# Other start addresses in SBUF for the pools of a decoder-layer kernel

## The chip, the cores and the metric

The kernel runs as one program on one core of a Trainium2 chip. The metric is device time in microseconds (us) of one execution, the median of several runs; lower is better. The core's engines are TensorE (PE: matmuls; PEld: its loads of the stationary operand), VectorE (DVE), ScalarE (ACT), GpSimd (POOL) and SyncE (SP, which issues the DMAs here).

## What is computed

One layer of a conditioned decoder on 256 tokens of 2048 channels, all in float32. Both halves are normalised (RMS norm) and shifted, scaled and gated by vectors made from a conditioning vector `c`:

```python
mod = silu(c) @ w_ada + b_ada                       # 2048 x 12288
h = rms_norm(x) * (1 + scale1) + shift1
z = h @ w_in + b_in                                 # 2048 x 11312: q, k, v, gates, GLU
y_attn = nsa_attention(q, k, v, gates) @ w_nsa_out  # compressed, selected and window branch
y_conv = conformer_conv(a_glu)                      # causal depthwise convolution of 31 taps, pointwise
x = x + gate1 * ((g0 * y_attn + g1 * y_conv) @ w_out)
h2 = rms_norm(x) * (1 + scale2) + shift2
s = (h2 @ w_q) . sub_keys; choose 16 of 16384 experts for each of 8 heads
out = x + gate2 * sum_e gate_e * gelu(h2 . u_e) * v_e
```

The kernel does the last line densely: `h2` against all 16384 rows of `u`, then the coefficients (zero where an expert is not chosen) against all rows of `v`. So nearly all of its work is one long row of matrix products whose weights (512 KB a transfer, some 500 MB in all) come from HBM once.

## The kernel before

**The stream of weights.** The class `Stream` (L130 to L217) takes the weights chunk by chunk. A chunk is 1024 float32 columns of each of 128 partitions. SP loads it into one of four tiles `raw` (L147). For each half of it, a piece of 512 columns, ACT writes the rounded part `hi` (L153, type float32r) and DVE the rest `lo = raw - hi` (L159, float32r); there are five `hi` and four `lo` tiles. `raw`, `hi` and `lo` are the pool `stream`.

**The products of a piece.** What is multiplied is split in the same way, so a product is three matmuls: high x high, high x low, low x high. In the projections (L200 to L202) the weights are the stationary operand (128x128, loaded by PEld) and the activations, 256 tokens, are the moving one: twelve matmuls of 256 columns a piece. In the stage of `u` (L213, L215) high and low part of `h2` lie side by side and are moved together, 512 columns, against `hi`, then the high part alone, 256 columns, against `lo`: eight matmuls a piece. In the stage of `v` (L1310 to L1312) it is the other way round: the coefficients `chi`, `clo` are stationary and 512 columns of `hi` or `lo` are moved: six matmuls a piece. Rows of the profile name the output, then the moving operand, then the stationary one: `acc<-hhi,lo` moves `hhi` over the stationary `lo`.

**The order of the work.** It is written out by hand (`manual_schedule`). `Stream.piece` (L170) keeps the splits up to three pieces ahead of the products, issues the products and then lets each job that runs beside them take a step or a fraction of one: the convolution, the adaLN vectors (`ada_steps`, which loads 256 KB tiles `adaw` and sums them on DVE, L383), the norms, attention, the top-16 search, the scatter of the gates.

**The stages** by the moving operand on PE, in us of the trace: 0 to 148 shift, scale and norm, with plain float32 products (`zb<-hr,w`, L339, no split); 148 to 561 projections of `h` (`hhi`, `hlo`) with convolution, then attention beside them; 561 to 645 `yhi`, `ylo`; 645 to 834 `ohi`, `olo` and the last of `h` in turn, with the adaLN jobs; 834 to 939 the output projection of `mhi`, `mlo`; 939 to 1037 `uhi`, `ulo` and then `h2` against the query weights of the experts; 1037 to 1794 `h2` against `u`; 1794 to 2501 the stage of `v`.

**Memory.** Pools are laid out as they are opened: `const`, `stream` and others from the low end of a partition upwards, those with `side="right"` from the high end downwards. A tile starts at the next multiple of 32 bytes. No address is written in the kernel; sizes and order give them.

Of the kernel before, what the change touches and what calls it, by code (L numbers as in the profile page):

```python
# [9 lines left out]
F32 = mybir.dt.float32  # L10
# [23 lines left out]
BIG = 1e30  # L34
# the gates are split into two halves of 11 bits, exactly, after this factor
GS = 32768.0
LOW = -3.0e38

# columns of the packed vectors
VEC = {}  # L40
# [7 lines left out]

# columns of the constants
CID, CONE, CMASK, CIOTA, CCM, CVAL, CI16, CEPS = 0, 128, 256, 384, 512, 542, 543, 559  # L50
# [22 lines left out]
def build(nc, tc, d):  # L73
# [18 lines left out]
    const = P("const")  # L92
    stream = P("stream")
    dram = ctx.enter_context(tc.tile_pool(name="dram", bufs=1, space=DRAM))
    ctx.enter_context(tc.manual_schedule())
# [21 lines left out]
    def col_sum(ps, a):  # L117
        """ps[m, :] = sum over partitions of a[:, m], in each of 128 columns."""
        pe.matmul(ps, a, ones, start=True, stop=True)
# [4 lines left out]

    # ---- the stream of weights: 4 KiB chunks of each partition, split exactly into high and
    # low parts in pieces of 512 columns, ahead of the products ----
    AHEAD = 3

    class Stream:
# [11 lines left out]
        def prefetch(self, to):  # L141
            """Low parts up to piece `to`, high parts up to the next one."""
            last = 2 * len(self.chunks) - 1
# [21 lines left out]
        def piece(self, mm):  # L165
            """The products of the next piece, and a step of each job that runs beside them."""
            self.prefetch(self.at + AHEAD)
            mm(*self.parts.pop(self.at))
            self.at += 1
            self.step()  # L170
# [10 lines left out]
        def add(self, gen, rate=1.0):  # L181
            """A job: `rate` steps of it beside each piece."""
            job = [gen, rate, 0.0]
            self.jobs.append(job)
            return job
# [7 lines left out]
        def proj(self, bank, nk, xhi, xlo, evac):  # L193
            """ps[n, t] = sum_k W[k, n] x[k, t] with the next chunks of the stream."""
            ps = bank()
            for k0 in range(0, nk, 4):
                def mm(hi, lo):
                    for j in range(4):
                        k, o = k0 + j, j * 128
                        pe.matmul(ps, hi[:, o:o + 128], xhi[:, k], start=(k == 0), stop=False)  # L200
                        pe.matmul(ps, hi[:, o:o + 128], xlo[:, k], start=False, stop=False)  # L201
                        pe.matmul(ps, lo[:, o:o + 128], xhi[:, k], start=False, stop=(k == nk - 1))  # L202
                self.piece(mm)
            return self.add(evac(ps))

        def proj2(self, bank, nk, x, evac):
            """The same with x = [high | low]; ps[:, 0] + ps[:, 1] are the sums."""
            ps = bank()
# [16 lines left out]
    G0, G1, QT, GATE = 43, 59, 27, 26  # L225
    # row tiles of v that are taken bank by bank
    LAST = 8
# [25 lines left out]

# [1 line left out]
    sp.dma_start(vec, d["vec"])  # L255
# [12 lines left out]

    # silu(c); halved biases for sigmoid through tanh: gate, glu (16), merge gates (32), all from b_gate on
    ctmp = const.tile([128, 16], F32, name="ctmp")  # L270
# [4 lines left out]
    ve.tensor_scalar(hvec, vec[:, g0:g0 + 49], 0.5, None, op0=OP.mult)  # L275
    gkq = const.tile([128, 3], F32, name="gkq")
    ve.tensor_scalar(gkq, v("gk", 0, 3), v("gq"), None, op0=OP.mult)

# [14 lines left out]
    def first_h(k):  # L293
        """shift1, scale1 and h of 128 channels."""
        acc = xp.tile([128, 2, 256], F32, name="acc1", tag="acc1", bufs=2)
# [40 lines left out]
    def first_z(k):  # L336
        """Their share of the first column tiles."""
        for n in range(14):
            pe.matmul(zb[n // 2][:, n % 2], ws[k][n // 7][:, n % 7], hr[k], start=(k == 0 and n % 2 == 0),  # L339
                      stop=(k == KT - 1), skip_group_check=True)  # L340
# [14 lines left out]

# [1 line left out]
    adap = [None]  # L357

    def ada_steps(groups, bank):
        """mod columns of groups of 512 channels."""  # L360
        pool = adap[0]
# [42 lines left out]

# [1 line left out]
    cpool = P("cpool", side="right")  # L406
# [54 lines left out]
    def conv_steps():  # L461
# [11 lines left out]
        yield  # L473
        # by tokens: mean and variance of the channels, from transposes
        yT = glu.rearrange("p c t -> p (c t)")[:, 0:2 * CT * 128].rearrange("p (a b) -> p a b", a=4)
# [62 lines left out]

    # keys and values
    adap[0] = P("adap")  # L540
# [19 lines left out]
    def gelu_small(out, ps):  # L560
        # 0.5 x (1 + tanh(sqrt(2/pi) (x + 0.044715 x^3)))
        x = cp.tile([64, 128], F32, name="gx", tag="gx", bufs=2)[0:60]
# [67 lines left out]
    def sums_steps(src, o, step):  # L630
        """By token: the sums of src[:, token]^2 over the partitions, into ssq[:, o + half * step]."""
        p2 = gen_bank([128, 2, 128])
# [33 lines left out]
    def q_evac(h):  # L666
        def f(ps):
# [4 lines left out]
            yield  # L672
            # columns by group, query tile, head
            yield from sums_steps(q, (h // 4) * 8 + h % 4, 4)
# [37 lines left out]

    # 1/sqrt of the mean squares of the keys; of the queries, with the scale of the scores
    def k_norm_steps():
# [26 lines left out]

# [1 line left out]
    P.close("gpool", "cp")  # L743
# [5 lines left out]
    def attention(g, qt):  # L749
# [25 lines left out]

        # compressed keys
        pk = gen_bank([128, HPG, NG, 24])
# [10 lines left out]
        yield  # L788
        # selected blocks (all of them) and window
        maxima(0, s0)  # L790
# [16 lines left out]
        yield  # L807
        # gate / sum
        ve.reciprocal(sums, sums)
# [50 lines left out]

    # the convolution's projection
    def conv_out(n):
# [30 lines left out]

# [1 line left out]
    ada[1] = 0.9  # L895
# [19 lines left out]

# [1 line left out]
    # h2 = rs2[t] u + shift2 with u = x1 (1 + scale2) g2; the first projections take u and, as two more  # L917
    # columns, shift2, since u needs no sum over all channels
    UC = T + 2
# [5 lines left out]
    rs2 = np_.tile([128, T], F32, name="rs2")  # L925
    hgate = np_.tile([128, 16], F32, name="hgate")
    uhi = np_.tile([128, KT, UC], F32R, name="uhi")
    ulo = np_.tile([128, KT, UC], F32R, name="ulo")
    x1d = dram.tile([128, 2, D], F32, name="x1d")
    ss2 = np_.tile([128, 2, 4], F32, name="ss2")  # L930
    r2 = np_.tile([128, 2], F32, name="r2")
    summed = []

    def x1_out(q):
        """Four channel tiles of x1, by tokens, to DRAM."""
        for tt in range(2):
# [32 lines left out]
    def h2_steps():  # L969
        """The columns of shift2; then rs2 and h2."""  # L970
        while not summed:
# [42 lines left out]

# [1 line left out]
    def u_bank(shape, tag, bufs=2):  # L1016
# [25 lines left out]
    def pairs(gen):  # L1042
        """Two steps of a generator as one."""
        while next(gen, S) is not S:
# [49 lines left out]
    def top_steps():  # L1094
        for h in range(PH):
            while h not in heads:
                yield
            yield from head_top(heads[h], h)
        # softmax of the chosen scores
        G4 = [128, 2, PH, TOPK]  # L1100
# [8 lines left out]
        yield  # L1109
        # slots on partitions  # L1110
        for nm, src in (("I1T", I1), ("I2T", I2), ("low", gates)):
# [77 lines left out]
    def g_steps():  # L1189
        """The gates of four tokens at a time, scattered over all experts and into C."""  # L1190
        I1T, I2T, high, low = (slot_t[n] for n in ("I1T", "I2T", "high", "low"))
# [64 lines left out]
    def coef(i1):  # L1256
        """The parts of an expert row tile's coefficients."""
        if i1 <= HALF:
# [10 lines left out]

# [1 line left out]
    coefs = {0: coef(0)}  # L1271
# [5 lines left out]
    def gate2_steps():  # L1277
        """The terms of gate2, by rows of w_ada."""
        todo = [(g, k) for g in range(4) for k in range(KT)]
# [37 lines left out]
    def gate2_sums():  # L1317
        """The first sums to SBUF; gate2 of all tokens through their banks."""
        for tt in range(2):
# [43 lines left out]
    S.finish(end)  # L1363
    P.close("ps_mix", "vp", "gg", "cb", "stream", "const")
    ctx.close()


def layout(inputs):
    """The inputs in the order in which the chip reads them."""
    a = {n: np.asarray(x) for n, x in inputs.items()}  # L1370
# [5 lines left out]
    def tiles(w, nk):  # L1376
        # [K, N] -> [N/128][128 k][nk][128 n]
        n = w.shape[1] // 128
# [22 lines left out]
    wa = a["w_ada"][0]  # L1401
    # by 128 channels: [channel tile][row within its tile][row tile][shift, scale][channel]
    wa1 = wa[:, 0:4096].reshape(KT, 128, 2, KT, 128).transpose(3, 1, 0, 2, 4).reshape(KT, 128, KT, 256)
# [27 lines left out]
```

## Time and profile before

| | |
|---|---|
| three runs | 2503.33, 2505.09, 2512.18 us (median 2505.09) |
| profiled execution, first to last instruction | 2506.6 us |
| busy share | PE 98%, PEld 86%, DVE 78%, ACT 57% |
| DMA | 540 MB, mean 216 GB/s |
| granted PE clock | 0.998 of full speed (mean) |
| chain that ended last | PE 86%, DMA 6%, DVE 6% |

The three runs and the span of the profiled execution lie within 0.4% of each other. How to read it: "busy" of PE overlaps from one matmul to the next, since matmuls are pipelined and their ends are modelled; what a matmul really takes of PE's time is the distance from its start to the start of the next one in the timeline.

### The profile page before, as it was taken

Reading aid. Unit: us, or ns where it says so; the run is one execution under the profiler, and the core shown is the slowest. Engines: PE = TensorE matmul, PEld = TensorE weight load, DVE = VectorE, ACT = ScalarE, POOL = GpSimd, SP = SyncE. Lnnn points to the kernel's source line nnn. Section 1 sums busy time; section 2 is a strip of 40 time slices with the busy share of each in tenths; the row PEclk is TensorE's granted clock in tenths of the full one; section 3 lists DMA queues with packets and bytes.
Section 4 is the critical chain, followed back from the end, with each engine's and each line's share of the span. In section 5 each row is a group of like instructions: output and inputs, shape, how many; then the busy total and the mean of one; then the engine's idle time right before and its main releaser. Section 6 shows DMA issues by size and latency. Waiting matters only on the chain.

```text
span 2506.6 us, 44063 instructions
## 1 busy us (share of the span) xinstructions
PE 2456.7 (98%) x15324; PEld 2165.1 (86%) x15324; DVE 1944.4 (78%) x4136; ACT 1421.1 (57%) x3198; POOL 0.2 (0%) x4
## 2 busy tenths in 40 slices
PE   7999999999999999999999999999999999999999
PEld 6899999888989999988888888888888888888887
DVE  7979886888777876899987888888655556666665
ACT  1045456776444456555568888887555555555554
POOL 0000000000000000000000000000000000000000
PEclk9999999999999999999999999999999999999999
DMA  9955566645988885555555555555555557777766
GB/s 382 395 190 194 178 194 196 202 155 188 308 288 289 291 280 194 177 185 186 190 183 175 175 173 173 176 170 176 185 191 190 192 190 253 243 237 241 238 208 195
DMA packets 171553, 540.48 MB, mean 216 GB/s; under 512 B 18753, under 2 KB 19009, under 8 KB 171073
## 3 DMA queue, kind: packets, MB, share of 16 engines
q1 hardware_dynamic: 171330, 537.67, 64.9%
q8 instruction: 120, 1.97, 0.3%
q14 instruction: 103, 0.84, 0.1%
HBM read 533.41 MB, written 4.19 MB: 214 GB/s over the span
## 4 chain that ended last, share of the span: by engine, by line
PE 86%; DMA 6%; DVE 6%; issue 1%; SPq 0%; ACT 0%; DVEq 0%
PE ps_acc L213 19%; PE ps_acc L215 10%; PE acc L200 7%; PE acc L202 7%; PE acc L201 7%; DMA adaw<-in_w_ada_dram 5%; DVE acc L307 2%; PE ps_o L1312 2%; PE ps_t L1312 2%; PE ps_s L1312 2%; PE ps_acc L1312 2%; PE ps_o L1311 2%; PE ps_s L1311 2%; PE ps_t L1311 2%; PE ps_acc L1311 2%; PE ps_o L1310 2%
## 5 line engine op out<-in xcount | busy, mean ns | idle before, releaser
L153 ACT CAST hi<-raw 128x512 fp32r<-128x512 f32 x1548 | 954.4, 621 | 835.3 <-PE acc L201 237.0
L159 DVE TENSOR_TENSOR lo<-raw,hi 128x512 fp32r<-128x512 f32 x1548 | 1062.2, 688 | 389.3 <-ACT hi L153 79.9
L213 PE MATMUL ps_acc<-h,hi 128*128 128x512 f32 x2048 | 731.3, 400 | 0.0
L215 PE MATMUL ps_acc<-h,lo 128*128 128x256 f32 x2048 | 575.1, 281 | 0.0
L213 PEld LDWEIGHTS ps_acc<-h,hi 128*128 128x128 f32 x2048 | 385.2, 188 | 91.1
L215 PEld LDWEIGHTS ps_acc<-h,lo 128*128 128x128 f32 x2048 | 384.7, 188 | 0.0
L200 PE MATMUL acc<-hhi,hi 128*128 128x256 f32 x1200 | 347.0, 289 | 0.0
L202 PE MATMUL acc<-hhi,lo 128*128 128x256 f32 x1200 | 335.0, 279 | 3.4 <-DVE lo L159 3.1
L201 PE MATMUL acc<-hlo,hi 128*128 128x256 f32 x1200 | 334.2, 278 | 0.0
L200 PEld LDWEIGHTS acc<-hhi,hi 128*128 128x128 f32 x1200 | 225.8, 188 | 6.3 <-issue 5.3
L202 PEld LDWEIGHTS acc<-hhi,lo 128*128 128x128 f32 x1200 | 226.2, 188 | 5.2 <-DVE lo L159 5.2
L201 PEld LDWEIGHTS acc<-hlo,hi 128*128 128x128 f32 x1200 | 226.3, 189 | 3.2 <-issue 3.1
L383 DVE SCALAR_TENSOR_TENSOR ada<-adaw,sc_c,ada 128x512 f32<-128x512 f32 x180 | 134.4, 747 | 51.4 <-DMA adaw<-in_w_ada_dram 51.3
L469 DVE SCALAR_TENSOR_TENSOR cacc<-glu,dwh,cacc 128x256 f32<-128x256 f32 x240 | 105.3, 476 | 0.0
L1202 ACT ACTIVATE Ahi<-ohA,high 128x128 f16<-128x128 f16 x256 | 100.5, 392 | 0.0
L339 PE MATMUL zb<-hr,w 128*128 128x256 f32 x448 | 100.4, 382 | 0.0
L1202 ACT ACTIVATE Alo<-ohA,low 128x128 f16<-128x128 f16 x256 | 99.0, 387 | 0.0
L339 PEld LDWEIGHTS zb<-hr,w 128*128 128x128 f32 x448 | 85.0, 192 | 11.1
L307 DVE SCALAR_TENSOR_TENSOR acc<-wa,sc_c,acc 128x256 f32<-128x256 f32 x224 | 91.4, 477 | 0.0
L202 PE MATMUL acc<-ohi,lo 128*128 128x256 f32 x256 | 72.7, 284 | 6.8 <-DVE lo L159 6.7
L202 PE MATMUL acc<-mhi,lo 128*128 128x256 f32 x256 | 73.6, 287 | 3.2 <-DVE lo L159 3.2
L200 PE MATMUL acc<-mhi,hi 128*128 128x256 f32 x256 | 73.1, 286 | 0.0
(367 smaller groups left out, 4388.3 us busy)
## 6 DMA issues: line engine op xcount, KB each, us to landing
raw<-in_u_dram SPq DMA_DIRECT2D x256, 512.0 KB, 3.7
raw<-in_v_dram SPq DMA_DIRECT2D x256, 512.0 KB, 4.4
raw<-in_w_in_dram SPq DMA_DIRECT2D x150, 512.0 KB, 4.2
adaw<-in_w_ada_dram SPq DMA_DIRECT2D x192, 256.0 KB, 5.4
wa<-in_w_ada_dram SPq DMA_DIRECT2D x64, 512.0 KB, 9.2
raw<-in_nsa_out_dram SPq DMA_DIRECT2D x32, 512.0 KB, 5.3
raw<-in_w_out_dram SPq DMA_DIRECT2D x32, 512.0 KB, 5.4
raw<-in_peer_wq_dram SPq DMA_DIRECT2D x32, 512.0 KB, 3.7
```

Source lines behind the costliest of these rows:

```text
L153: sc.copy(hi, self.source(n))
L159: ve.tensor_sub(lo, self.source(n), hi.bitcast(F32))
L200: pe.matmul(ps, hi[:, o:o + 128], xhi[:, k], start=(k == 0), stop=False)
L201: pe.matmul(ps, hi[:, o:o + 128], xlo[:, k], start=False, stop=False)
L202: pe.matmul(ps, lo[:, o:o + 128], xhi[:, k], start=False, stop=(k == nk - 1))
L213: pe.matmul(ps.rearrange("p a t -> p (a t)"), hi[:, o:o + 128], x[:, k].rearrange("p a t -> p (a t)"), start=(k == 0), stop=False)
L215: pe.matmul(ps[:, 1], lo[:, o:o + 128], x[:, k, 0], start=False, stop=(k == nk - 1))
L307: ve.scalar_tensor_tensor(a, raw[:, i], c, a, op0=OP.mult, op1=OP.add)
L339: pe.matmul(zb[n // 2][:, n % 2], ws[k][n // 7][:, n % 7], hr[k], start=(k == 0 and n % 2 == 0), stop=(k == KT - 1), skip_group_check=True)
L1202: sc.activation(part[:, j], A[:, j], AF.Copy, scale=g[:, t0 + j:t0 + j + 1])
L1311: pe.matmul(ps, chi, lo, start=False, stop=False)
L1312: pe.matmul(ps, clo, hi, start=False, stop=(i1 == NK - 1))
```

## The change

It inserts or moves small tiles so that pools start elsewhere. No instruction is added, taken out or moved: on PE, DVE, ACT, POOL and SP the two built programs have the same instructions in the same order with the same waits; they differ in the addresses of their operands (and in line numbers, since comment lines were dropped too).

- `fill`, 32 bytes in `const`, moves the pool `stream` behind it by 32 bytes.
- `between`, a pool of 64 bytes right behind `stream`, moves the pools above it by 96 bytes in all.
- `edge`, a pool of 96 bytes at the high end, moves all pools of the right side down by 96 bytes.
- `hgate` (64 bytes) now stands behind `uhi` and `ulo` instead of in front of them.

```diff
     const = P("const")
     stream = P("stream")
+
+    between = P("between")
+    between.tile([128, 16], F32, name="between")
+    edge = P("edge", side="right")
+    edge.tile([128, 24], F32, name="edge")
     dram = ctx.enter_context(tc.tile_pool(name="dram", bufs=1, space=DRAM))
...
     gkq = const.tile([128, 3], F32, name="gkq")
+    const.tile([128, 8], F32, name="fill")
     ve.tensor_scalar(gkq, v("gk", 0, 3), v("gq"), None, op0=OP.mult)
...
     rs2 = np_.tile([128, T], F32, name="rs2")
-    hgate = np_.tile([128, 16], F32, name="hgate")
     uhi = np_.tile([128, KT, UC], F32R, name="uhi")
     ulo = np_.tile([128, KT, UC], F32R, name="ulo")
     x1d = dram.tile([128, 2, D], F32, name="x1d")
+    hgate = np_.tile([128, 16], F32, name="hgate")
...
-    P.close("ps_mix", "vp", "gg", "cb", "stream", "const")
+    P.close("ps_mix", "vp", "gg", "edge", "cb", "between", "stream", "const")
```

The start addresses (bytes in a partition) in the two built programs, of the first tile of each name, with the remainder modulo 128:

| tile | role on PE | before | after |
|---|---|---|---|
| `raw` (4 x 4096 bytes) | none | 22048: 32 | 22080: 64 |
| `hi` (5 x 2048), `lo` (4 x 2048) | stationary; moving in the stage of `v` | 38432, 48672: 32 | 38464, 48704: 64 |
| `hhi`, `hlo` | moving | 196576, 212960: 96 | 196480, 212864: 0 |
| `yhi`, `ylo`; `ohi`, `olo` | moving | 96 | 0 |
| `mhi`, `mlo` | moving | 85536, 101920: 32 | 85632, 102016: 0 |
| `uhi`, `ulo` (rows of 258 columns: channel tile k starts 1032 k bytes further) | moving | 146080, 162592: 32 | 145920, 162432: 0 |
| `h2` | moving | 188384: 96 | 188288: 0 |
| `chi`, `clo` (and `ohA`, `ohB`, `Ahi`, `Alo` in their place) | stationary | 174048, 183264: 96 | 173952, 183168: 0 |
| `wa`, `w` (first stage), `adaw` | none; `w` stationary | 32 | 0 |
| `glu`, `cacc` | none | 139200: 64, 148352: 0 | 139104: 96, 148256: 32 |

Before, every float32r operand of PE but `uhi` and `ulo` starts 32 bytes behind a multiple of 64. Afterwards all of them but the later channel tiles of `uhi` and `ulo` start on a multiple of 64. The distance from moving to stationary operand modulo 128 is 64 before in all stages but that of `mhi` (0) and `uhi` (8 k), and 64 afterwards in all but that of `uhi` (64 + 8 k).

## Rows read from the trace of the kernel before

**Rows 1.** Page, part 1: engine, busy us (share of the span), instructions.
```profile
PE 2456.7 (98%) x15324; PEld 2165.1 (86%) x15324; DVE 1944.4 (78%) x4136; ACT 1421.1 (57%) x3198; POOL 0.2 (0%) x4
```

**Rows 2.** Windows: stretch, us, busy (instructions) by engine, granted clock, DMA share, GB/s.
```profile
0.00:148.00 148.00, 125.90 (x605) 107.92 (x605) 125.98 (x349) 22.35 (x49) 0.20 (x4) 0.97 0.94 363
148.00:430.00 282.00, 279.94 (x2361) 273.07 (x2360) 240.66 (x517) 156.92 (x321) 0.00 (x0) 1.00 0.58 186
645.00:834.00 189.00, 174.58 (x1465) 169.18 (x1464) 146.49 (x253) 87.46 (x198) 0.00 (x0) 1.00 0.90 296
834.00:939.00 105.00, 99.13 (x805) 96.54 (x805) 84.65 (x150) 53.31 (x124) 0.00 (x0) 1.00 0.88 282
1037.00:1150.00 113.00, 113.00 (x645) 98.33 (x645) 104.86 (x312) 63.61 (x121) 0.00 (x0) 1.00 0.56 185
1150.00:1794.00 644.00, 644.00 (x3980) 557.04 (x3980) 540.69 (x1246) 472.75 (x1224) 0.00 (x0) 1.00 0.55 177
1794.00:2501.00 707.00, 707.00 (x3083) 578.33 (x3081) 447.48 (x719) 358.32 (x642) 0.00 (x0) 1.00 0.67 216
```

**Rows 3.** Timeline of PE: start us, us, engine, instruction, count; first stage.
```profile
139.80 6.42 PE L339 MATMUL zb<-hr,w 128*128 128x256 f32 x29
```

**Rows 4.** Timeline of PE, 165 to 180: projections of h, early.
```profile
164.76 0.28 PE L200 MATMUL acc<-hhi,hi 128*128 128x256 f32 x1
...
179.96 0.28 PE L200 MATMUL acc<-hhi,hi 128*128 128x256 f32 x1
```

**Rows 5.** Timeline of PE, 325 to 331: projections of h, later.
```profile
324.73 0.28 PE L201 MATMUL acc<-hlo,hi 128*128 128x256 f32 x1
...
330.96 0.28 PE L202 MATMUL acc<-hhi,lo 128*128 128x256 f32 x1
```

**Rows 6.** Timeline of PE, 898 to 904: output projection.
```profile
897.83 0.28 PE L202 MATMUL acc<-mhi,lo 128*128 128x256 f32 x1
...
903.95 0.28 PE L202 MATMUL acc<-mhi,lo 128*128 128x256 f32 x1
```

**Rows 7.** Timeline of PE, 1260 to 1275: stage of u.
```profile
1259.83 0.40 PE L213 MATMUL ps_acc<-h,hi 128*128 128x512 f32 x1
...
1274.67 0.40 PE L213 MATMUL ps_acc<-h,hi 128*128 128x512 f32 x1
```

**Rows 8.** Timeline of PE, 2300 to 2320: stage of v.
```profile
2299.65 0.39 PE L1310 MATMUL ps_o<-hi,chi 128*128 128x512 f32 x1
...
2319.79 0.39 PE L1311 MATMUL ps_t<-lo,chi 128*128 128x512 f32 x1
```

**Rows 9.** Page, part 5: instructions, shapes, count, busy us, mean ns, idle before.
```profile
L213 PE MATMUL ps_acc<-h,hi 128*128 128x512 f32 x2048 | 731.3, 400 | 0.0
...
L200 PE MATMUL acc<-hhi,hi 128*128 128x256 f32 x1200 | 347.0, 289 | 0.0
...
L469 DVE SCALAR_TENSOR_TENSOR cacc<-glu,dwh,cacc 128x256 f32<-128x256 f32 x240 | 105.3, 476 | 0.0
...
L339 PE MATMUL zb<-hr,w 128*128 128x256 f32 x448 | 100.4, 382 | 0.0
...
L307 DVE SCALAR_TENSOR_TENSOR acc<-wa,sc_c,acc 128x256 f32<-128x256 f32 x224 | 91.4, 477 | 0.0
```

**Rows 10.** Waits: who waited for whom, us in total, times, longest.
```profile
ACT hi L153 <- PE ps_acc L213: 195.4, 298, 1.3
...
DVE ada L383 <- DMA adaw<-in_w_ada_dram: 51.3, 44, 5.0
...
PE acc L202 <- DVE lo L159: 12.9, 21, 2.2
```

## The prediction

> **What bounds the kernel now.** I read the busy shares first: PE 98%, DVE 78%, ACT 57% [rows 1]. PE's figure alone says little, since a matmul's modelled end overlaps the next start. The windows by stage come second [rows 2]: from 1037 to 2501, 58% of the span, PE has no gap, DMA is busy for about 0.6 of the time, and DVE's share is 0.93, then 0.84, then 0.63. Third, the waits say who is early [rows 10]: ACT waits 195 us for PE's matmuls of the stage of `u`, since a `hi` tile comes free only with them, while PE waits 13 us for `lo` in the whole run. [...]
>
> Fourth, the timelines of PE, in which I count starts. All these matmuls have a fresh 128x128 load behind each:
> - Plain float32, 256 columns: 29 in a row, 28 steps in 6.42 us less the last one's own 0.38 [rows 9], so 216 ns [rows 3].
> - float32r, 256 columns, `hhi`/`hlo`: 129 steps in 15.20 us, 117.8 ns [rows 4]; in a later stretch 55 steps in 6.23 us, 113.3 ns [rows 5].
> - The same shape with `mhi`/`mlo`: 51 steps in 6.12 us, 120.0 ns [rows 6].
> - `u`: 42 pairs (512 + 256 columns) in 14.84 us, 353.3 ns a pair [rows 7].
> - `v`: 88 steps of 512 columns in 20.14 us, 228.9 ns [rows 8].
>
> [...] The same instruction takes 117.8 in one stretch and 113.3 in another, and always 120.0 for the one tensor that starts at the same remainder modulo 128 as its weights. Nothing differs between rows 4, 5 and 6 in shape; what differs is where the tiles lie, and how the load and the matmul fell in step after the last interruption.
>
> **A reading of these numbers (an estimate).** [...] If PE fetches whole 64-byte lines, no faster than it eats them, an off-line start costs one line per 256 columns. [...] The rest, up to 120.0, would be the load of the stationary operand meeting the moving one in the same half of 128 bytes: worst at distance 0 (rows 6), less at 64 (rows 4, 5). The change puts all starts on lines and all distances but `uhi`'s at 64. No row shows a float32r matmul with both operands on a line, so the value has to be bounded.
>
> **The change part by part.**
> Instructions, order and waits are the same, so there is no issue cost and no new wait; the padding takes 160 bytes and none of it is read or written. What can change is only how long an access takes.
>
> *DVE and ACT: nothing.* The convolution's taps (L469) read `glu` at every multiple of 4 bytes and write `cacc` at remainder 0; the adaLN sums (L307) read and write at 32. Same operation, same 256 columns: 476 and 477 ns [rows 9]. These engines do not care where a tile starts.
>
> *DMA.* No row shows a weight transfer to another remainder. It matters where DMA sets the pace: 0 to 148 (share 0.94) and 645 to 939 (0.90 and 0.88, DVE waiting 51 us for `adaw` over the run) [rows 2, 10]. That is 148 x 0.94 + 189 x 0.90 + 105 x 0.88 = 402 us of transfer; 1% in its rate is 4 us either way. I take 0, with -4 to +8 in the range.
>
> *Stage of `u`.* 2048 pairs [rows 9]. A pair touches three times 256 columns, so three lines go: 20.0 ns, 353.3 to 333.3. 2048 x 20.0 = 41 us. [...]
>
> *Stage of `v`.* 512 pieces of six, 3072 matmuls. [...] Two lines each: 13.3 ns, 228.9 to 215.6, 41 us, which is also what the floor of 216 gives. Bounds: 0 and 41; with one line a run it would be 20 here and 27 in `u`.
>
> *Projections of `hhi`, `yhi`, `h2`.* `hhi` has 3 x 1200 [rows 9], of which 14 column tiles of 48 lie between 645 and 834; `yhi` and `h2` 384 each: 3600 - 672 + 768 = 3696 outside that stage. One line each: 3696 x 6.67 = 25 us. [...]
>
> *645 to 834.* DMA is at 0.90 and PE is busy 175 of 189 us, waiting for the chain from `adaw`: I count nothing (10 us if PE set it).
>
> *`mhi`, 834 to 939.* 768 x 6.67 = 5 us on PE, but PE has 6 us of idle time here and DMA 0.88: I take 2. If only the distance matters and not the line, 768 x (120.0 - 115.6, the middle of rows 4 and 5) = 3 us is the whole effect.
>
> *`uhi`.* Its channel tiles step by 1032 bytes, so all remainders by 8 occur before and after, and 258 columns touch 17 lines either way: 0.
>
> *The cover that goes.* A faster PE meets DVE. 1037 to 1150: DVE 104.9 of 113 us; with PE at 333.3/353.3 the stage would be 106.6, DVE at 98%: I give back 3 us. 148 to 430: DVE 240.7 of 282, PE 16 us shorter, DVE at 90%: back 2. 1150 to 1794: DVE 540.7 in 607, 89%: back 3. In `v` DVE stays at 447 of 666. Together 8.
>
> **Sum.** 41 + 41 + 25 + 2 - 8 = 101 us. The page gives the span, 2506.6 us, 1.5 above the median of the three runs, so the same is taken off: 2506.6 - 101 - 1.5, rounded to 2405 us. With the upper bounds for `u` and the projections (17 and 6 more) it is 2382; with half of the saving kept, 2455.
>
> **The rivals.**
> 1. *Starts do not matter, only the distance or nothing.* For: rows 4 and 5 differ by 4.5 ns at the same addresses, so some of the loss has to do with how load and matmul fall in step, and the distance stays 64 in most stages. [...] Then `mhi` alone gains, 3 us: 2502. [...]
> [...]
> 3. *The other side: PE falls into the worse step.* One mechanism: with both starts on lines, load and moving reads begin in phase and collide as in rows 6, at 120.0 per 256 columns, in every stage. `u` 2048 x (360.0 - 353.3) = 14 us, `v` 3072 x (240.0 - 228.9) = 34, projections 3696 x 4.4 = 16: 2569. It decides from the point where the pair of `u` takes more than 353.3 ns. For: distance 0 modulo 64 is common to rows 4 and 6, so 64 may not be the safe distance I take it for. Against: rows 4 and 6 do differ.
> 4. *DMA pays.* Transfers slow down and PE gains nothing. [...] By rows alone: 402 us of transfer where DMA sets the pace, and 2% on it, the most I allow, are 8 us: 2513.
>
> **How the numbers follow.** The 64-byte reading holds, 2380 to 2455: 0.42. Rival 2: 0.18. Rival 1: 0.21. Rival 4: 0.04. Rival 3, or a part of it: 0.15. A measurement of this kernel tells 0.5%, 12.5 us, from no change. Faster: 0.42 + 0.18 and a little of rival 1 where DMA gains as well, 0.62. Slower: 0.15. Same: 0.23. The range reaches from 2370 (the upper bounds and some DMA gain) to 2515, which takes in rivals 1, 2 and 4 and leaves out most of rival 3. The likeliest case has 2380 to 2455 alone.
>
> **What would show it.** In the changed kernel's timeline: pairs of `u` at 333 ns or less, `v` at 216, 256-column projections at 107 to 110 in all stages, and `uhi` near its old pace. L469 and L307 at 476 and 477 whatever their new remainders. ACT's wait for PE in `u` shrinks and PE's wait for `lo` grows. I am wrong if 113.3 stays the floor (starts don't matter), if pairs of `u` exceed 353 (rival 3), or if PE is faster but DVE's or DMA's stages give the time back.

## The result, and the profile after

The changed kernel takes 2527.31 us (median) against 2506.24 us for the kernel before on the same chip: ratio 1.0079, 95% interval [1.0062, 1.0095]. It is slower by 0.8%, where 2405 us was forecast and up to 2515 allowed for. One of the four runs of the changed kernel, 6903.54 us at a granted clock of 0.352 of full speed, is left out of the ratio; the other three took 2525.90, 2526.88 and 2527.74 us.

The profiled execution spans 2525.1 us, 18.5 more than before. The page, part 1 (against [rows 1]): PE takes 21 us more, DVE and ACT stay within 1.3 us.

```profile
PE 2477.6 (98%) x15324; PEld 2175.9 (86%) x15324; DVE 1944.6 (77%) x4136; ACT 1422.4 (56%) x3198; POOL 0.2 (0%) x4
```

The windows by stage, same columns and the same stages as [rows 2], of which each begins up to 6 us later:

```profile
0.00:149.00 149.00, 128.63 (x611) 110.22 (x612) 126.09 (x351) 23.51 (x52) 0.20 (x4) 0.95 0.94 360
149.00:430.00 281.00, 280.07 (x2345) 273.59 (x2345) 238.38 (x511) 154.94 (x315) 0.00 (x0) 1.00 0.57 185
649.00:838.00 189.00, 176.62 (x1467) 173.31 (x1466) 146.00 (x252) 88.03 (x198) 0.00 (x0) 0.99 0.90 295
838.00:944.00 106.00, 98.52 (x804) 94.80 (x803) 85.36 (x150) 53.58 (x124) 0.00 (x0) 1.00 0.87 282
1043.00:1150.00 107.00, 107.00 (x612) 93.25 (x611) 99.04 (x296) 60.12 (x114) 0.00 (x0) 1.00 0.56 186
1150.00:1799.00 649.00, 649.00 (x4015) 563.19 (x4014) 546.56 (x1262) 476.02 (x1230) 0.00 (x0) 1.00 0.55 177
1799.00:2519.00 720.00, 720.00 (x3082) 578.74 (x3081) 446.82 (x719) 358.80 (x642) 0.00 (x0) 1.00 0.66 213
```

From the ends of the stages: up to 645 before and 649 now, +4; 645 to 834 is 189 us in both; 834 to 939 becomes 838 to 944, +1; the stage of `u` with the query projections ahead of it (`uhi`, `ulo` and `h2`), 939 to 1794, is 855 us in both (944 to 1799); the stage of `v`, 707 us, becomes 720, +13. That is 18 of the 18.5 us. In `u` and `v` PE still has no gap, and DMA's share is the same or 0.01 lower in every window.

The pace in the stage of `v`, first and last start of a stretch of PE's timeline with 86 steps between, none missing:

```profile
2299.71 0.40 PE L1316 MATMUL ps_s<-hi,chi 128*128 128x512 f32 x1
...
2319.78 0.40 PE L1318 MATMUL ps_acc<-hi,clo 128*128 128x512 f32 x1
```

20.07 us / 86 = 233.4 ns, where [rows 8] had 228.9. Over all undisturbed steps of the stage the mean is 233.33 against 228.92; 3072 x 4.41 = 13.5 us, the stage's 13.

In the stage of `u`, 42 pairs:

```profile
1259.88 0.39 PE L218 MATMUL ps_acc<-h,hi 128*128 128x512 f32 x1
...
1274.72 0.39 PE L218 MATMUL ps_acc<-h,hi 128*128 128x512 f32 x1
```

14.84 us / 42 = 353.3 ns a pair, just as [rows 7]. Later in the stage groups of pairs at 348.6 to 349.2 come between those at 353 and 354; the mean is 352.3 against 353.0, 1.3 us over 2048 pairs.

The projections of `h`, early (129 steps) and later (55 steps):

```profile
164.73 0.28 PE L206 MATMUL acc<-hlo,hi 128*128 128x256 f32 x1
...
179.92 0.28 PE L206 MATMUL acc<-hlo,hi 128*128 128x256 f32 x1
```

```profile
324.75 0.28 PE L206 MATMUL acc<-hlo,hi 128*128 128x256 f32 x1
...
330.99 0.28 PE L207 MATMUL acc<-hhi,lo 128*128 128x256 f32 x1
```

117.8 and 113.5 ns: the two paces of [rows 4, 5], at the same places. What changed is how often each is met. In groups of 12 steps without a gap between 150 and 640 us, the first dozen steps after each interruption left out, 50 groups ran at 113.3 and 64 at 117.8 before; now 20 and 92. The mean of the steps below 135 ns goes from 115.5 to 117.2, some 5 us over the 2928 matmuls of `h` outside the stage from 645 to 834, in which DMA is busy for 0.90 of the time.

Page part 5 and waits, against [rows 9, 10]: DVE's two operations take 476 and 478 ns after 476 and 477, ACT's casts to `hi` 621 ns in both (the line of the kernel before stands first), and these three waits differ from before by 2.2 us at most.

```profile
L153 ACT CAST hi<-raw 128x512 fp32r<-128x512 f32 x1548 | 954.4, 621 | 835.3 <-PE acc L201 237.0
...
L158 ACT CAST hi<-raw 128x512 fp32r<-128x512 f32 x1548 | 955.2, 621 | 854.4 <-PE acc L206 239.7
...
L218 PE MATMUL ps_acc<-h,hi 128*128 128x512 f32 x2048 | 730.2, 398 | 0.0
...
L475 DVE SCALAR_TENSOR_TENSOR cacc<-glu,dwh,cacc 128x256 f32<-128x256 f32 x240 | 105.2, 476 | 0.0
...
L313 DVE SCALAR_TENSOR_TENSOR acc<-wa,sc_c,acc 128x256 f32<-128x256 f32 x224 | 91.2, 478 | 0.0
```

```profile
ACT hi L158 <- PE ps_acc L218: 193.2, 298, 1.3
...
DVE ada L389 <- DMA adaw<-in_w_ada_dram: 53.1, 45, 5.2
...
PE acc L207 <- DVE lo L164: 13.2, 17, 2.5
```

### The profile page after: what moved, and what is told of

It reads as the page before. It is cut to its first block, busy times and chain, and to the rows that moved or that the text cites. A ratio compares the mean times of both kernels' runs of the same rounds, so it can differ in the third digit from the quotient of the medians.

```text
span 2525.1 us, 44063 instructions
## 1 busy us (share of the span) xinstructions
PE 2477.6 (98%) x15324; PEld 2175.9 (86%) x15324; DVE 1944.6 (77%) x4136; ACT 1422.4 (56%) x3198; POOL 0.2 (0%) x4
## 4 chain that ended last, share of the span: by engine, by line
PE 87%; DVE 6%; DMA 5%; issue 1%; SPq 0%; ACT 0%; DVEq 0%; ACTq 0%
PE ps_acc L218 19%; PE ps_acc L220 10%; PE acc L205 7%; PE acc L207 7%; PE acc L206 7%; DMA adaw<-in_w_ada_dram 4%; DVE acc L313 3%; PE ps_o L1318 2%; PE ps_t L1317 2%; PE ps_s L1318 2%; PE ps_t L1316 2%; PE ps_s L1316 2%; PE ps_o L1316 2%; PE ps_s L1317 2%; PE ps_t L1318 2%; PE ps_o L1317 2%
## 5 line engine op out<-in xcount | busy, mean ns | idle before, releaser
L389 DVE SCALAR_TENSOR_TENSOR ada<-adaw,sc_c,ada 128x512 f32<-128x512 f32 x180 | 134.5, 747 | 53.1 <-DMA adaw<-in_w_ada_dram 53.1
L206 PE MATMUL acc<-mlo,hi 128*128 128x256 f32 x256 | 71.5, 279 | 1.0 <-DVE mlo L911 1.0
```

## The experiments

Below, the distance of a matmul is the start of its moving operand less that of its stationary one, in bytes of the partition, modulo 256. "Settled" paces are means of start-to-start steps, worked out from all starts of the trace, without the first steps after an interruption. In the code and the edits below, `...` marks what is left out; the edits that put in a pool also name it where the pools are closed.

**Every start on a grid of 8 bytes (`grid256`).** The layer is left out; TensorE alone streams 256 columns of float32r under a fresh 128x128 load.

```
for s in range(0, 32, 2):          # stationary start, 8-byte steps over 128
    for m in range(0, 32, 2):      # moving start
        reset()
        for n in range(36):
            a, b = s + (n % 4) * 128, m + (n % 4) * 256
            pe.matmul(acc, sta[:, a:a + 128], mov[:, b:b + 256], start=(n == 0), stop=(n == 35))
```

> This kernel leaves the whole layer out: PE alone runs float32r matmuls of 256 columns, each with its own 128x128 load, 36 for each of 16 x 16 pairs of starts, stationary and moving operand at 0, 8, ..., 120 bytes modulo 128, with two plain float32 matmuls between pairs; no other engine works. Line theory (the prediction's): starts at 0 and 64 of the moving operand give 107 to 110 ns, all others 113 or more. Distance theory: the time depends on (moving - stationary) modulo 128 alone, so it is equal along the diagonals, worst (120) at 0 and best at 64. Step theory (the two streams lock in one of a few steps, and the address only decides in which): times between 113.3 and 120 at all starts, 0 and 64 no exception, with no order by distance.

Two cells from PE's timeline (start us, us, 36 matmuls each): both starts 0, and stationary 0 with moving 64.

```profile
25.84 4.55 PE L47 MATMUL acc<-mov,sta 128*128 128x256 f32 x36
...
63.60 4.33 PE L47 MATMUL acc<-mov,sta 128*128 128x256 f32 x36
```

The first step takes 200 ns in both; the last 24 are 120.0 ns in the one cell and 113.3 in the other. Settled paces at multiples of 32 bytes:

```
stationary \ moving    0      32     64     96
 0                   120.0  116.7  113.3  120.0
32                   118.3  120.0  116.7  117.8
64                   113.3  118.3  119.9  116.7
96                   118.5  113.3  118.3  120.0
```

No cell of the 256 goes below 113.3, and of the four with both starts on a 64-byte line two are at 113.3 and two at 120. 113.3 also appears with starts off the line (stationary 96, moving 32; stationary 8, moving 48), and the slowest cells take some 123, above the 120 that the step theory had as the top. So the 64-byte line, the ground of my forecast, is refuted. But (32, 96) and (96, 32) differ by 4.5 ns at the same distance of 64 modulo 128, so that was not the right measure either.

**The kernel's own shapes, and further multiples of 128 bytes (`far_shapes`).** The layer is left out; `u`'s pairs, `v`'s 512 columns and 256 columns, with starts 0, 32, 64, 96 and the moving start 0 to 896 bytes further in steps of 128.

```
for far in range(0, 256, 32):
    for s in (0, 8, 16, 24):
        for m in (0, 8, 16, 24):
            ...                        # reset, the pairs, reset
            for n in range(24):
                a, b = s + (n // 6 % 2) * 128, m + far + (n % 3) * 512
                pe.matmul(acc, sta[:, a:a + 128], mov[:, b:b + 512], start=(n == 0), stop=(n == 23))
            ...                        # reset, 256 columns
```

> This kernel leaves the whole layer out: PE alone runs, for stationary and moving starts of 0, 32, 64, 96 modulo 128 and further distances in steps of 128 bytes up to 896, the pairs of the stage of u (512 and 256 columns), the 512-column matmuls of the stage of v, and 256-column ones. Line theory: both starts at 0 or 64 give pairs of 325 to 333 and 216 for 512 columns. Distance theory: equal distances modulo 128 give equal times, and steps of 128 change nothing. Step theory: the pair takes 340 to 360 and 512 columns 226 to 240 everywhere, and steps of 128 bytes may change a time as much as steps of 32.

Three cells of 24 matmuls of 512 columns (start us, us): distance 0, then 64 (stationary 0, moving 64), then 192 (stationary 64, moving 0).

```profile
31.50 5.71 PE L58 MATMUL acc<-mov,sta 128*128 128x512 f32 x24
...
62.07 5.75 PE L58 MATMUL acc<-mov,sta 128*128 128x512 f32 x24
...
154.07 5.85 PE L58 MATMUL acc<-mov,sta 128*128 128x512 f32 x24
```

The second and third have the same starts, exchanged, and differ by 0.10 us in 23 steps, 4.4 ns each. The settled paces repeat every 256 bytes, to 0.1 ns, and change at 128; the absolute start makes hardly a difference for 512 columns:

```
distance  512 columns   u's pair             256 columns
  0       226.7         346.6 or 353.9       120.0
 32       233.3         346.7                116.7
 64       228.9         348.6 or 352.9-354   117.8
 96       233.3         350.0                120.0
128       231.7-232.9   350.8-351.8          118.2-120.0
160       234.2         346.7                117.1-118.6
192       233.3         353.3                117.8
224       233.3         346.7 or 353.3       118.2-118.8
```

(Where two values stand, cells at that distance fall into one or the other.) The distances of the kernels, from where their tiles lie: `v` 64 before and 192 after, `u` 192 before and 64 after, the projections of `h`, `y`, `o` and `h2` 192 and 64, `mhi` 0 and 64. So TensorE by itself gives the 228.9 and 233.3 of `v` and the 353.3 of `u` in [rows 7]. For the projections it does not give the difference: 117.8 at 192 as at 64. The change did not keep the distance at 64: it kept it only modulo 128.

**The fill alone (`fill_only`).** The weights move by 32 bytes, nothing else.

```
 gkq = const.tile([128, 3], F32, name="gkq")
+const.tile([128, 8], F32, name="fill")
```

> Only the 32 bytes in the constants: stream and left pools at 64 modulo 128, right pools still at 96, so h, h2, chi are 32 from their partner instead of 64, and mhi stays at distance 0 (now on a line). Distance theory: u and v leave both 353 and 228.9, toward the 119.5 per 256 columns that uhi shows on average: u 358, v 239, some 2545 to 2555 us. Line theory: one operand on a line, at most half of any effect: between 2506 and 2527. Step theory: any of 340 to 360 for u and 226 to 236 for v, 2490 to 2530, and w_out as before at 120 only by chance.

2517.57 us, ratio 1.0040 [1.0025, 1.0055]. The distances are `u` 160 and `v` 96; by the table 346.6 and 233.3. The kernel's timelines, 44 pairs of `u` and 87 steps of `v`:

```profile
1259.64 0.39 PE L213 MATMUL ps_acc<-h,hi 128*128 128x512 f32 x1
...
1274.89 0.39 PE L213 MATMUL ps_acc<-h,hi 128*128 128x512 f32 x1
```

```profile
2299.61 0.39 PE L1311 MATMUL ps_s<-hi,chi 128*128 128x512 f32 x1
...
2319.91 0.39 PE L1311 MATMUL ps_acc<-hi,chi 128*128 128x512 f32 x1
```

346.6 and 233.3 ns. This half of the change makes `u` faster by 6 ns a pair and `v` slower by 4.4 a matmul, which nearly cancel. The 10 us come mostly from the projections: those of `h`, at a distance of 160, take 118.0 ns for 115.5, 9 us over 3600. The time is below the 2545 to 2555 of the distance modulo 128; the ranges of the line theory and of the step theory both hold it.

**The 96 bytes at the right alone (`edge_only`).** All other pools move, the weights stay.

```
 stream = P("stream")
+edge = P("edge", side="right")
+edge.tile([128, 24], F32, name="edge")
...
```

> Only the 96 bytes at the high end: right pools at 0 modulo 128, stream and left pools still at 32, so h, h2, chi stand at 96 from their partner instead of 64; mhi as before. Distance theory: as with the fill alone, 2545 to 2555, w_out at 120 as before. Line theory: the moving operand of u and of the projections is on a line and gains if lines count at all: u at most 340. Step theory: u 340 to 360, v 226 to 236, 2490 to 2530, not the same as with the fill alone.

2531.10 us, ratio 1.0092 [1.0076, 1.0109]. Distances: `u` 96, `v` 160; by the table 350.0 and 234.2. 43 pairs and 86 steps:

```profile
1259.74 0.39 PE L215 MATMUL ps_acc<-h,hi 128*128 128x512 f32 x1
...
1274.79 0.39 PE L215 MATMUL ps_acc<-h,hi 128*128 128x512 f32 x1
```

```profile
2299.66 0.40 PE L1314 MATMUL ps_s<-hi,clo 128*128 128x512 f32 x1
...
2319.81 0.39 PE L1313 MATMUL ps_acc<-lo,chi 128*128 128x512 f32 x1
```

350.0 and 234.3 ns, and 119.9 in the projections of `h`, at a distance of 96. The time is below the 2545 of the distance modulo 128 and 1 us above the 2530 of the step theory, and `u` is above the 340 of the line theory. The two halves have different patterns and don't add up to the change: each distance has its own pace.

**Both distances to their best (`near`).** From the table: `v` to 0, `u` to 160, the projections of `h`, `y` and `o` left at 192.

```
+gpad = P("gpad", side="right")
+gpad.tile([128, 48], F32, name="gpad")
 gg = P("gg", side="right")
+hpad = P("hpad", side="right")
+hpad.tile([128, 24], F32, name="hpad")
 h2p = P("h2p", side="right")
...
```

> The kernel before with two unused pools of 192 and 96 bytes, so that g and the token operands of u move and nothing else. Moving start minus stationary start, modulo 256 bytes: v 64 becomes 0, u 192 becomes 160; modulo 128 bytes: v 64 becomes 0, u 64 becomes 32. No start lies on a 64-byte line. Distance modulo 256: v 228.9 becomes 226.7 ns (-2.2 x 3072 = -7 us), the u pair 353.3 becomes 346.6 (-6.7 x 2048 = -13.7 us), so about 2485 us. Line theory: as before, 2506 us, since all starts stay off the lines. Only the step that PE falls into, by chance: within 10 us of before.

2489.47 us against 2505.05, ratio 0.9938 [0.9925, 0.9952]: faster than both kernels, with all starts off the 64-byte lines. 43 pairs of `u` and 89 steps of `v`:

```profile
1259.92 0.39 PE L213 MATMUL ps_acc<-h,hi 128*128 128x512 f32 x1
...
1274.82 0.39 PE L213 MATMUL ps_acc<-h,hi 128*128 128x512 f32 x1
```

```profile
2299.82 0.39 PE L1315 MATMUL ps_o<-lo,chi 128*128 128x512 f32 x1
...
2319.99 0.39 PE L1314 MATMUL ps_acc<-hi,chi 128*128 128x512 f32 x1
```

346.5 and 226.6 ns; over the stages 346.7 and 226.75. The windows of the two stages (with the query projections in the first):

```profile
944.00:1788.00 844.00, 844.00 (x5458) 751.66 (x5458) 716.55 (x1730) 595.73 (x1464) 0.00 (x0) 1.00 0.55 182
1788.00:2488.00 700.00, 700.00 (x3082) 578.15 (x3081) 447.18 (x719) 359.15 (x642) 0.00 (x0) 1.00 0.67 219
```

844 and 700 us instead of 855 and 707: 18 us, of 2048 x 6.3 + 3072 x 2.2 = 19.7; the query projections of `h2`, which this edit moves to 160 as well, went the other way, from 115.5 to 118.5 ns, 1 us over 384. In this execution 4 us are lost in the stage that waits for DMA, 193 us instead of 189.

**The change, 128 bytes further in `v` and `u` alone (`after128`).**

```
 UC = T + 2
+gpad = P("gpad", side="right")
+gpad.tile([128, 32], F32, name="gpad")
 gg = P("gg", side="right")
...
```

> The changed kernel with one unused pool of 128 bytes in front of g and the token operands of u. Every start stays on a 64-byte line and every distance modulo 128 bytes stays as in the changed kernel. Distance modulo 256: v 192 becomes 64, its matmul 233.3 becomes 228.9 ns (-4.4 x 3072 = -13.5 us); u 64 becomes 192, its pair 352.3 becomes 353.3 (+2 us): about 2515 us, half of the loss undone. Line theory and distance modulo 128: no change, 2527 us.

2512.97 us, ratio 1.0026 [1.0013, 1.0039]. 88 steps of `v`:

```profile
2299.76 0.39 PE L1318 MATMUL ps_t<-hi,chi 128*128 128x512 f32 x1
...
2319.90 0.39 PE L1319 MATMUL ps_o<-lo,chi 128*128 128x512 f32 x1
```

228.9 ns: 128 bytes, which change neither a start's place in a 64-byte line nor a distance modulo 128, give 13 of the 20 us back. What stays, 0.26% or 6.5 us, fits the projections' share: `h` still stands at 64 and takes 117.2 ns, 6 us more than 115.5 over 3600.

**The change with everything at the right 128 bytes further (`line_back`), and the kernel before with those 128 bytes alone (`only128`).** A cross of the two theories: on the lines with the distances of before, and off the lines with those of after.

```
-edge.tile([128, 24], F32, name="edge")     # line_back, in the changed kernel
+edge.tile([128, 56], F32, name="edge")
+edge = P("edge", side="right")             # only128, in the kernel before
+edge.tile([128, 32], F32, name="edge")
...
```

> The changed kernel with its 96-byte pool at the right made 224 bytes, so that everything on that side stands 128 bytes further. Every start that the change put on a 64-byte line stays on one; the distances modulo 256 bytes become those of the kernel before: v 64, u 192, the projections, y, o and h2 192 (they were 192, 64 and 64). Distance modulo 256: v 228.9, u pair 353.3, h 115.5 ns, and the whole loss goes: 2506 us, within 5 us of before. Line theory and distance modulo 128: no change, 2527 us.

> The kernel before with one unused pool of 128 bytes at the right and no other edit: no start comes onto a 64-byte line, every distance modulo 128 bytes stays. Distances modulo 256 become those of the changed kernel: v 192, u 64, the projections, y, o and h2 64. Distance modulo 256: v 233.3, u pair 352.3, h 117.2 ns, about 2527 us, the whole loss of the change without the change. Line theory and distance modulo 128: no change, 2506 us.

`line_back`: 2508.05 us, ratio 1.0008 [0.9998, 1.0019]. 88 steps of `v`:

```profile
2299.80 0.39 PE L1317 MATMUL ps_acc<-lo,chi 128*128 128x512 f32 x1
...
2319.94 0.39 PE L1318 MATMUL ps_t<-hi,clo 128*128 128x512 f32 x1
```

`only128`: 2522.60 us, ratio 1.0063 [1.0039, 1.0087]. 86 steps of `v`:

```profile
2299.78 0.39 PE L1314 MATMUL ps_o<-hi,clo 128*128 128x512 f32 x1
...
2319.84 0.39 PE L1313 MATMUL ps_t<-lo,chi 128*128 128x512 f32 x1
```

228.9 and 233.3 ns. On the lines with the old distances nothing is left of the loss (`u` 353.0, `h` 115.3); off the lines with the new ones the loss is there without the change (`u` 352.3, `h` 117.1), 0.6% where 0.8% was expected, and the intervals overlap. That settles it: the loss comes from the distance modulo 256 bytes, and the place in the line has no part in it that these runs could tell. For the projections it is the kernels that show it, not TensorE alone: `h` takes 115.5, 115.6 and 115.3 ns in the three with a distance of 192 (before, `near`, `line_back`), and 117.2, 117.2 and 117.1 in the three with 64 (the change, `after128`, `only128`).

**Does the load collide with the moving read? (`widths`, `pairs`).** The layer is left out. `widths` puts loads of 128, 96, 64 and 32 columns under 256 moving ones, and then runs `v`'s three products with the starts of all operands varied; `pairs` does that for `u` and the projections.

```
for w in (128, 96, 64, 32):
    for m in range(0, 64, 8):
        reset()
        for n in range(24):
            a, b = (n % 4) * 128, m + (n % 4) * 256
            pe.matmul(acc[0:w, 0:256], sta[:, a:a + w], mov[:, b:b + 256], start=(n == 0), stop=(n == 23))
...
```

> Leaves out the whole layer: TensorE alone runs 256 moving columns with 128, 96, 64 and 32 stationary ones loaded under them at eight distances, and v's three products of 512 columns with the starts of g's two parts and of the low weights in 32-byte steps over 256 bytes. If the load's reads collide with the moving reads, the excess over 113.3 ns falls as the load narrows, to about a quarter at 32 columns (120.0 to about 115). If only the starts count, the width changes nothing. v: 226.7 ns where every product has distance 0, up to 234 elsewhere.

Four cells (start us, us): loads of 128 columns at distance 0 and 192, of 32 columns at 0 and 192.

```profile
25.54 3.11 PE L49 MATMUL acc<-mov,sta 128*128 128x256 f32 x24
...
45.27 2.98 PE L49 MATMUL acc<-mov,sta 128*128 128x256 f32 x24
...
103.87 3.07 PE L49 MATMUL acc<-mov,sta 128*32 128x256 f32 x24
...
123.49 2.99 PE L49 MATMUL acc<-mov,sta 128*32 128x256 f32 x24
```

Settled paces, distances 0 to 224 in steps of 32:

```
128 columns: 119.8 116.7 117.8 119.9 118.6 117.4 113.3 118.4
 96 columns: 116.1 116.7 117.8 117.6 119.2 116.8 117.4 117.9
 64 columns: 113.3 118.6 116.6 116.7 116.7 116.9 118.9 116.7
 32 columns: 117.8 117.2 116.6 117.5 120.0 117.9 113.4 117.5
```

A load of a quarter of the columns leaves paces between 113.4 and 120.0, as the full one does. The excess does not shrink with the load, so a plain count of colliding reads is not the cause; but the width does move the pace at a distance (0: 119.8 at 128 columns, 113.3 at 64, 117.8 at 32), so the load seems to have a part in it. The runs do not show that alone, since a narrower load also writes fewer partitions of the output. With all of `v`'s products at distance 0 the settled pace was 226.7, the least of its 512 cells; others went up to 236.7, where 234 was expected.

> Leaves out the whole layer: TensorE alone runs u's pairs of 512 and 256 columns (high part's stationary start 0, the low part's and the moving start in 32-byte steps over 256 bytes) and the projections' three products. Distance modulo 256: the pair is 346.6 ns wherever both distances are 32 or 160, and a pair whose two products have unlike distances lies between their own values; the three products have a least mean near 113.3 to 116 ns at some triple of starts, below the 115.5 of the kernel before. Line theory: least where all starts are 0, 64, 128 or 192. Only chance: no order by start.

`pairs`: 346.6 at distances 32 and 160 as before. The least, 340.0, has the high part's distance at 64 and the low part's at 0, which is below what either gives alone, so "between their own values" was wrong. The projections' least is 113.3, in two cells of 512; one has distance 192 in all three products, as the kernel before. Nearly all others lie between 115.5 and 120, a few up to 121.7. That is the 113.3 of [rows 5], which the changed kernel mostly lost. Distance 192 doesn't guarantee it, though: alone it gave 117.8 in `far_shapes` and 113.3 in `widths`, and the kernel before ran 64 of 114 groups at 117.8.

## Why the prediction was wrong

**PE's pace as the time of `u` and `v`: right.** 4.41 ns more on each of 3072 matmuls lengthened the stage of `v` by 13 us, and in `near` 6.3 and 2.2 ns less shortened both stages by 18 of 20 us. Whether the 8 us for the cover that goes were right is not shown: no run gained anything near 100 us.

**The reading as whole lines of 64 bytes: the step that failed.** "If PE fetches whole 64-byte lines, ... an off-line start costs one line per 256 columns" carried 107 of the 109 us of the gain before give-back. Measured: `grid256` has 113.3 as the floor with both starts on lines, `line_back` stands on the lines and runs at before's time. "Two lines each: 13.3 ns, 228.9 to 215.6", -41 us in `v`, was +13.5; -41 in `u` was -1.3; -25 in the projections was about +6. No run shows the 6.67 ns that the sum takes for a line, the floor of 216 for `v`, or the 17 and 6 us of the upper bounds. In their place the runs show paces that go with the distance: 226.7 to 234.2 ns for 512 columns and 346.6 to 354 for the pair in `far_shapes`, and nothing below 113.3 for 256 columns in `grid256`. I took a guess for a mechanism though rows 4 and 5 showed two paces at one placement, which no count of lines alone gives.

**The distance, "64 afterwards": the step that gave the sign.** I counted it modulo 128 and so held it for unchanged. Modulo 256 it went from 64 to 192 in `v` and from 192 to 64 in `u` and the projections. `after128` undid it in `v` and `u` alone, 13 of 20 us, and `only128` made it everywhere but in `mhi` without the change. No row of before shows a period of the distance at all; 128 was the unit in which the change is worded, and I gave the case that it is another no chance of its own.

**`mhi`: 2 us on PE, as its distance alone would give.** From 119.7 to 117.1 ns a matmul, at distances of 0 and 64, for which `far_shapes` has 120.0 and 117.8. The stage got 1 us longer all the same: PE's idle time in it grew from 5.9 to 7.5 us, with DMA's share at 0.88 and 0.87; what PE waited for there was not followed up. `uhi` kept its pace, as forecast: 120.4 and 120.2 ns for 258 columns.

**DVE, ACT and DMA at nothing: right.** 476 and 478 ns on DVE and 621 on ACT at new starts, and 1944.4 and 1944.6 us busy on DVE, 1421.1 and 1422.4 on ACT, in all; DMA's share at most 0.01 off in each stage, DVE's wait for `adaw` 53.1 us after 51.3. The padding is 192 bytes and not 160, since `fill` has 32 as well; nothing hung on it.

**The rivals.** The first was right on its first half: the start alone does not matter, with `line_back` on the lines at 1.0008 of the time before. The third, the worse step, was nearest in its outcome and wrong in its mechanism: PE did fall into one, in `v` by 4.4 ns and not 11, and in the projections more often than before (117.2 ns on average, not 120), but `line_back` has both starts on lines without it and `only128` has it off the lines. Its decision point, a pair of `u` above 353.3, was not reached (352.3). The second, all matmuls at the 113.3 ns of rows 5, is what `near` has in part: `u` at 346.7, where three times 113.3 is 340, and `v` at 226.75, where twice is 226.7. The fourth did not occur.

**What stays open.** Why 256 bytes, and whether the load and the moving read meet there at all. In `far_shapes` TensorE takes 226.7 or 233.3 ns for the same instructions (distances 0 and 192) by the distance of the two operands alone; that the two reads share something or fall in step is my guess, and by `widths` the excess does not go in proportion to the columns loaded (113.4 to 120.0 ns with 32, 113.3 to 119.9 with 128). Nor do the runs show why TensorE alone holds 117.8 at 192 in one program (`far_shapes`) and 113.3 in another (`widths`).

## What to carry to other kernels

When PE has no gaps and its float32r matmuls, each with a fresh load, run some per cent above the best pace that TensorE alone showed (here 113.3 ns for 256 columns in `grid256`, 226.7 for 512 in `far_shapes`), the relative start of moving and stationary tiles is worth trying: measure the pace over distances modulo 256 bytes with TensorE alone and pad pools by 32 to 224 bytes; 0.6% came from 288 bytes here (`near`). Take the period from a measurement and not from the unit in which the change is worded. A change that pads one pool moves every distance to it: list them all, per product, before and after.

## What was not expected of the hardware

- The pace of float32r matmuls with fresh loads depends on the distance between the operands modulo 256 bytes: 226.7 to 234.3 ns for 512 columns (`far_shapes`, `edge_only`; up to 236.7 in `widths`, where three products have unlike distances), and for a pair of 512 and 256 from 340.0 (`pairs`) to 354 (`far_shapes`).
- Paces of 256 columns come back at a few values (113.3, 116.7, 117.8, 120.0) but are not confined to them: in `grid256` about a third of the cells are at 120.0, and the others lie between 113.3 and some 123. At one placement PE can hold two of them for tens of us (in the kernel before 117.8 from 149 to 219 us, then 113.4 and 117.7 in turn), and changed between them there at interruptions.
- No stream of 256 columns came below a settled 113.3 ns at any of the 256 start pairs of `grid256`.
